# Transposing keys and values by 32x32 blocks on VectorE and DMA instead of by products with the identity on TensorE

## The chip, the cores and the metric

The kernel runs on one core of one Trainium2 chip, whose engines are called here PE (TensorE, products), PEld (its weight loads), DVE (VectorE), ACT (ScalarE), POOL (GpSimd) and SP (SyncE). Each runs its own list of instructions in order. SP computes nothing; it issues the transfers between DRAM and the on-chip memory SBUF, or inside SBUF, which 16 DMA engines carry out. PE writes to PSUM, eight banks that DVE and ACT can read. The metric is the time of one launch in device microseconds (us), the median over the runs; lower is better.

## The reference

One layer of a language model on a sequence of 4096 positions with width 1024, and a final normalisation. Two groups of heads share one input projection: 4 heads of gated linear attention (GLA, key width 64, value width 128) and 8 heads of RWKV-7 (width 64). The code below is cut to what the change touches, the names are the reference's.

```
h = rmsnorm(x, norm_w);  u = h @ w_in            # 4096 x 1024, 1024 x 3728
# GLA, in chunks:  scores and the state of each head
scores  = einsum('id,jd->ij', q * exp(b), k * exp(-b))     # causal
o       = scores @ v + (q * exp(b)) @ S
S       = exp(b_last) * S + (k * exp(b_last - b)).T @ v
# RWKV-7, per position t and head (S: value x key)
S = S * w_t + (S @ -kk_t) (kk_t * a_t)^T + v_t^T k_t
y = S @ r_t
y = groupnorm(y);  y = y + sum(r * k * r_k) * v
out = rmsnorm(x + concat(gla * silu(gate), y * silu(gate)) @ w_out)
```

A product on PE sums over the partition axis (the 128 rows of SBUF). Projections give q, k, v with channels as rows and positions as columns. For the states the sum runs over positions, so keys and values are needed the other way round, with positions as rows. These are the transposes that the change is about.

## The kernel before, in words

The sequence is cut into 8 blocks of 512 positions. In a block the 8 RWKV heads are 4 units of two heads (128 channels), the 4 GLA heads are 2 pairs of two heads; so there are 32 units and 16 pairs in all. Each unit has 8 chunks of 64 positions, each pair 4 chunks of 128.

The program is written as generators, called streams: x (loads and normalises a block of x), w (splits the weights at the start), a (the RWKV units up to their chains), i (the rest of a unit's triangular inverse), c (the chains over the chunks, which carry the state), p and g (GLA's projections and pairs), o (the output projection of a block). A recorder (class Engine, `call` at L626, `duo` at L685) writes down every instruction that a stream makes; in the profile almost all instructions therefore carry one of these two lines, and they are told apart by engine and tile names. A planner then gives each instruction a place on its engine: `first_guide` (L227) unpacks the table STARTS into one start time for each recorded step of each stream (COUNTS tells how many a stream has), `build` runs the streams in the order of these times, and `forward` and `backward` (L450, L518) lay the steps out with the durations of `cost` (L546), counting at most 8 transfers in flight. At the end the steps are emitted in the order of their starts, each engine's as one list. So the order of all engines hangs on that table, on the durations, and on what waits for what. All transfers named here are issued by SP from one list.

One unit (`rwkv_ab`, L1084) does this. It projects the key input (rk), makes the decays, the normalised key and kf (the key with its factor), and projects r. From these it builds bk: 128 channels x 8 chunks x 128 columns, which hold k and the removal key of a chunk side by side. The products of bk with de and do, masked, give DD and Nb, the small matrices of each chunk. Nb's diagonal 32x32 blocks go out to DRAM (nd) and back as F (f in the profile), POOL inverts them in 62 steps on Tc and tm, and they return over DRAM (td) into Nb. Stream i (`rwkv_i`, L1234) then finishes the inverse with Ta. Meanwhile the unit projects v and the gate rg. Then come the transposes:

- bk, L1201 to L1208: eight products with the identity into two PSUM banks, four each, and two ACT copies of 128x512 back over bk.
- v, L1209 to L1220: four products with the identity into one bank; there DVE takes the sum of each position and head (vm) and takes the mean off (with no mean over a head's values, y has none either, which the group norm asks for), and four ACT copies of 64x256 put the result into sv.

`rwkv_c` (L1256) is the chain over the 8 chunks: three small products of PE for a chunk, on ch, with ACT's copies us and uv between them, and at the end of each link DVE writes the state for the next chunk into sv (`sv<-ch`). It reads Nb, the transposed bk, and sv.

A GLA pair (`gla_pair`, L1399) makes the factors bc and ep (tiles gbc and gep), multiplies them into qi and ki, and transposes ki by four products with the identity and one ACT copy into kt, which is the buffer of bc (L1434 to L1439). It then multiplies kt with vt for the change of the state (pd), uses ep's buffer for the states (sm), and later reuses kt's and ki's buffers for the squares (rss).

The tiles ta, kf, E, v, rk and rn exist once each and pass from unit to unit; bk and sv exist twice, the projection weights wr and wg in a few buffers each, refilled from DRAM (wdr) all the time.

```
T.transpose(f4(pt[c // 4])[:, c % 4, :], bk[:, c, :], ident)                  # L1203, bk
T.transpose(pv[:, c].rearrange("p h t -> p (h t)"), v[:, P * c:P * c + P], ident)   # L1213, v
T.transpose(pt[:, c, :], ki[:, c, :], ident)                                  # L1437, GLA
```

## Time and profile before

| | |
|---|---|
| time, median of 3 runs | 2201.78 us (2199.61 to 2207.04) |
| span of the profiled execution | 2206.1 us |
| mean granted PE clock in it | 0.993 |
| busy, PE | 2119.0 us, 96% |
| busy, PEld | 1352.7 us, 61% |
| busy, DVE | 1711.7 us, 78% |
| busy, ACT | 1253.8 us, 57% |
| busy, POOL | 875.1 us, 40% |
| DMA queue q1, share of 16 engines | 50.8% |

The profiled execution's span, from its first to its last instruction, is 2206.1 us; its own launch time is not told apart from the three above, the nearest of which is 2207.04 us. A row of instruction groups reads: line, engine, operation, the tile written <- the tiles read, shapes, xcount | busy us in all, mean ns of one | idle us of the engine just before them, and what ended that idle time. A row of a stretch reads: start:end length, then for PE, PEld, DVE, ACT and POOL the busy us and the count of instructions, the granted clock, the DMA share and GB/s. A row of waits reads: engine and tile that wait <- what they wait for: us in all, count, the longest. A row of the timeline reads: start, duration, what ran. "SPq" is SP issuing a transfer, "DMA" its travel to the landing. The engines overlap, so the busy times of one say nothing yet about the time of the launch.

### The profile page before, as it was taken

Reading aid. Unit: us, or ns where it says so; the run is one execution under the profiler, and the core shown is the slowest. Engines: PE = TensorE matmul, PEld = TensorE weight load, DVE = VectorE, ACT = ScalarE, POOL = GpSimd, SP = SyncE. Lnnn points to the kernel's source line nnn. Section 1 sums busy time; section 2 is a strip of 40 time slices with the busy share of each in tenths; the row PEclk is TensorE's granted clock in tenths of the full one; section 3 lists DMA queues with packets and bytes.
Section 4 is the critical chain, followed back from the end, with each engine's and each line's share of the span. In section 5 each row is a group of like instructions: output and inputs, shape, how many; then the busy total and the mean of one; then the engine's idle time right before and its main releaser. Section 6 shows DMA issues by size and latency. Waiting matters only on the chain.

```text
span 2206.1 us, 75003 instructions
## 1 busy us (share of the span) xinstructions
PE 2119.0 (96%) x30680; PEld 1352.7 (61%) x30680; DVE 1711.7 (78%) x3802; ACT 1253.8 (57%) x3229; POOL 875.1 (40%) x2212
## 2 busy tenths in 40 slices
PE   7888999999999999999999999999999999999997
PEld 3555665566755657556575666656666566756664
DVE  7888969688784977867877886867878578785876
ACT  7766675564645546554654546545465465555452
POOL 3454233625244352335525354441543525254400
PEclk9999999999999999999999999999999999999999
DMA  6786556455344643456444654355544465345443
GB/s 201 230 249 205 182 160 178 141 177 167 91 123 142 184 141 98 115 145 188 138 114 116 183 154 129 101 131 165 164 117 124 127 190 160 90 117 140 130 123 97
DMA packets 275454, 326.90 MB, mean 148 GB/s; under 512 B 131572, under 2 KB 132772, under 8 KB 275108
## 3 DMA queue, kind: packets, MB, share of 16 engines
q1 hardware_dynamic: 275108, 322.10, 50.8%
q8 instruction: 240, 3.93, 0.8%
q14 instruction: 106, 0.87, 0.1%
HBM read 276.94 MB, written 45.05 MB: 146 GB/s over the span
## 4 chain that ended last, share of the span: by engine, by line
PE 66%; DVE 16%; DMA 9%; issue 2%; ACT 2%; SPq 2%; POOL 2%; DVEq 0%; POOLq 0%; ACTq 0%
PE bank L685 52%; PE bank L626 8%; PE ch L685 4%; DMA xr<-in_xT_dram 2%; SPq L626 2%; DVE DD L626 2%; DVE nta L626 1%; DVE bk L626 1%; PE y L626 1%; DMA rn<-bcda 1%; DMA x<-in_wt_dram 1%; PE y L685 1%; DVE mgg L626 1%; DVE x L626 1%; DVE Nb L626 1%
## 5 line engine op out<-in xcount | busy, mean ns | idle before, releaser
L685 PE MATMUL bank<-x,wr 128*64 128x512 f16 x6528 | 796.2, 380 | 7.2 <-ACT x L626 1.4
L626 POOL TENSOR_TENSOR tm<-Tc,f 128x60 f32<-128x60 f32 (+24 forms) x961 | 347.7, 362 | 589.0 <-DMA f<-nd 507.2
L685 PEld LDWEIGHTS <-wr 128*64 128x64 f16 x6528 | 356.1, 110 | 260.1 <-issue 22.1
L626 POOL TENSOR_TENSOR Tc<-Tc,tm 128x60 f32<-128x60 f32 (+24 forms) x961 | 358.2, 373 | 74.1
L685 PE MATMUL bank<-x,wg 128*64 128x512 f16 x3072 | 367.1, 381 | 3.0 <-DMA wg<-wdr 1.9
L685 PE MATMUL bank<-x,wo 128*64 128x512 f16 x2976 | 357.2, 380 | 0.0
L626 POOL TENSOR_TENSOR xacc<-xacc,xr 128x512 f32<-128x512 f32 x98 | 130.8, 1334 | 359.5 <-ACT xr L626 227.9
L685 PEld LDWEIGHTS <-wg 128*64 128x64 f16 x3072 | 169.4, 110 | 126.3 <-issue 5.0
L626 DVE SCALAR_TENSOR_TENSOR sv<-ch,PC,psd 64x64 f32<-64x64 f32 x434 | 122.5, 282 | 160.1 <-PE ch L685 140.6
L685 PEld LDWEIGHTS <-wo 128*64 128x64 f16 x2976 | 159.2, 110 | 112.4 <-issue 2.9
L685 PEld LDWEIGHTS <-x 128*64 128x64 f16 x6240 | 190.1, 111 | 20.8 <-issue 9.0
L685 PE MATMUL bank<-wg,x 128*64 128x128 f16 x6144 | 195.4, 220 | 4.6 <-DMA wg<-wdr 3.0
L626 ACT ACTIVATE psd<-sv,PC 128x128 f32<-128x128 f32 x248 | 98.9, 399 | 139.4 <-DVE sv L626 108.3
L626 ACT COPY uv<-ch 64x64 f32<-64x64 f32 x496 | 102.3, 206 | 76.5 <-PE ch L685 69.5
L626 ACT COPY us<-ch 64x64 f32<-64x64 f32 x496 | 102.2, 206 | 67.8 <-PE ch L685 57.7
L626 ACT ACTIVATE sa<-bank,mu_s 128x512 f32<-128x512 f32 x104 | 71.6, 689 | 73.5 <-PE bank L685 71.1
L626 DVE COPY_PREDICATED Nb<-mc,bank 64x512 f32<-64x512 uint8 x128 | 92.8, 728 | 13.1 <-PE bank L626 11.3
L626 POOL MEMSET Tc<- 32x8 f32 (+1 forms) x160 | 24.2, 151 | 186.1 <-DMA td<-Tc 180.7
L626 DVE COPY_PREDICATED DD<-mc,bank 64x512 f32<-64x512 uint8 x128 | 93.3, 731 | 2.3
L685 PEld LDWEIGHTS ch<-uv,bk 128*64 128x64 f32 x992 | 66.1, 137 | 44.1 <-ACT uv L626 10.9
L685 PEld LDWEIGHTS ch<-us,Nb 128*64 128x64 f32 x992 | 65.4, 137 | 43.0 <-ACT us L626 11.0
L685 PEld LDWEIGHTS ch<-sv,DD 128*64 128x64 f32 x992 | 65.0, 136 | 40.0 <-DVE sv L626 7.3
(348 smaller groups left out, 3611.8 us busy)
## 6 DMA issues: line engine op xcount, KB each, us to landing
wr<-wdr SPq DMA_DIRECT2D x256, 256.0 KB
wg<-wdr SPq DMA_DIRECT2D x184, 256.0 KB
xr<-in_xT_dram SPq DMA_DIRECT2D x176, 256.0 KB
wo<-wdr SPq DMA_DIRECT2D x128, 256.0 KB
f<-nd SPq DMA_DIRECT2D x128, 128.0 KB
x<-in_wt_dram SPq DMA_DIRECT2D x29, 512.0 KB
wdr<-wo SPq DMA_DIRECT2D x25, 512.0 KB
out_dram<-mgg SPq DMA_DIRECT2D x33, 256.0 KB
```

The source lines that it names most:

```text
L626: put(t0, self.name, d, lag, cols, tiles, tab, outs, ins, lambda: f(*a, **kw))
L685: nc.tensor.matmul(x, lhsT=l, rhs=y, start=start, stop=stop)
```

## The change

Keys and values are transposed without PE. DVE's block transpose turns every 32x32 block of a tile and leaves the block where it stands; transfers then carry the blocks to where they belong.

- bk: right after the masked products of the unit, one block transpose of the whole bk (128x1024) into sv's buffer, four transfers of 128 KB from there to DRAM (kd, in pieces of 32 numbers), and one of 512 KB from DRAM over bk.
- v: one block transpose (128x512) into kf's buffer, and eight transfers of 32 KB inside SBUF into ta's buffer. The sum and the removal of the mean now work there instead of in PSUM, and two ACT copies of 64x512 put the result into sv.
- ki of GLA: one block transpose into ep's buffer, four transfers of 64 KB to DRAM (gd) and one of 256 KB over bc's buffer.
- `cost` gets a duration for the larger block transposes, and the tables COUNTS and STARTS are replaced.

```diff
--- before.py
+++ after.py
@@ -53,143 +53,140 @@
 PASSES = 5
 PUT_OFF = 1.0
 ROUNDS = (LOOKS,) * 1
-COUNTS = ((('d', 0), 19), (('d', 1), 19), (('d', 10), 19), (('d', 11), 19), (('d', 12), 19),
+COUNTS = (('a', 9713), ('c', 3379), ('e', 109), ('g', 1736), ('i', 1184), ('init', 38), ('o', 2464),
 STARTS = (
...
 )
 GUP = 2.0 ** 19
 DECAY = math.exp(-0.5)
@@ -560,6 +557,8 @@
                     runs = 0.126
                 elif n == 256 and half:
                     runs = 0.122 if op == "transpose" else 0.09
+                elif op == "transpose":
+                    runs = n * 0.00037
                 elif n == 512 and half:
                     runs = 0.115
                 elif op == "tensor_scalar" and few > 1:
@@ -1157,6 +1156,14 @@
             rel("r")
             hot.pop()
 
+            sv = sb(un, [P, NC, 2, 64], F32, "sv", 2)
+            sw = sv.rearrange("p c e t -> p (c e t)")
+            V.transpose(sw, bk.rearrange("p c t -> p (c t)"))
+            kd = sb(dr, [4, 32, NC, 4, 32], F32, "kd", 2)
+            for a in range(4):
+                D.dma_start(kd[:, :, :, a].rearrange("b i c t -> i c b t"), sw[32 * a:32 * a + 32].rearrange("p (c b t) -> p c b t", b=4, t=32))
+            D.dma_start(bk.rearrange("p c t -> p (c t)"), kd.rearrange("b i c a t -> (b i) (c a t)"))
+
             F = sb(rt, [P, 1024], F32, "f4", 1).rearrange("p (k t) -> p k t", k=32)
             nd = sb(dr, [4, NC, 32, 32], F32, "nd", 2)
             for q in range(4):
@@ -1198,26 +1205,20 @@
                 stat_mm(pst, bones, r)
                 add_bonus(pst[:, 0:P], *bonus.pop())
                 rel("r")
-            pt = yield from need("r", 2)
-            for c in range(NC):
-                T.transpose(f4(pt[c // 4])[:, c % 4, :], bk[:, c, :], ident)
-                if c == 3:
-                    yield now[0]
-            for i in range(2):
-                S.copy(bk[:, 4 * i:4 * i + 4, :], f4(pt[i]))
-            rel("r")
             yield after(v)
-            sv = sb(un, [P, NC, 2, 64], F32, "sv", 2)
-            pv = (yield from need("r")).rearrange("p (c h t) -> p c h t", c=4, h=2)
-            for c in range(4):
-                T.transpose(pv[:, c].rearrange("p h t -> p (h t)"), v[:, P * c:P * c + P], ident)
+            x, vt = tA("kf"), tA("ta")
+            V.transpose(x, v)
+            vt = f3(vt)
+            for a in range(4):
+                for s in range(2):
+                    o = 64 * (a < 2) + 32 * s
+                    D.dma_start(vt[o:o + 32, :, 32 * (a % 2):32 * (a % 2) + 32],
+                                x[32 * a:32 * a + 32].rearrange("p (c s t) -> p c s t", s=2, t=32)[:, :, s])
             vm = sb(rt, [P, 8, 1], F32, "vm", 1)
-            pu = pv.rearrange("p c h t -> p (c h) t")
-            V.tensor_reduce(vm, pu, op=ALU.add, axis=AX.X)
-            V.scalar_tensor_tensor(pu, vm.broadcast_to((P, 8, 64)), -1.0 / 64, pu, ALU.mult, ALU.add)
-            for k, q in enumerate((lo, hi)):
-                for e, o in enumerate((hi, lo)):
-                    S.copy(sv[o, k::2, e, :], pv[q, :, e, :])
+            V.tensor_reduce(vm, vt, op=ALU.add, axis=AX.X)
+            V.scalar_tensor_tensor(vt, vm.broadcast_to((P, 8, 64)), -1.0 / 64, vt, ALU.mult, ALU.add)
+            for e, o in enumerate((hi, lo)):
+                S.copy(sv[o, :, e, :], vt[o])
             units[u] = (DD[u % NBUF], nb, sv, bk, PC, bv, tg)
             done["A"] += 1
 
@@ -1430,14 +1431,15 @@
             done["GE"] += 1
             yield lambda: done["GV"] > n
             ki, qi, vt = g["ki"], g["qi"], g["vt"]
-            kt, sm = bc, ep
+            sm = ep
             yield after(ki)
-            pt = f4((yield from need("G")))
-            for c in range(4):
-                T.transpose(pt[:, c, :], ki[:, c, :], ident)
-            S.copy(kt, pt)
-            rel("G")
-            yield after(kt, vt)
+            xt, kt = ep.rearrange("p c t -> p (c t)"), bc
+            V.transpose(xt, ki.rearrange("p c t -> p (c t)"))
+            gd = sb(dr, [4, 32, 4, 4, 32], F32, "gd", 2)
+            for a in range(4):
+                D.dma_start(gd[:, :, :, a].rearrange("b i c t -> i c b t"), xt[32 * a:32 * a + 32].rearrange("p (c b t) -> p c b t", b=4, t=32))
+            D.dma_start(kt.rearrange("p c t -> p (c t)"), gd.rearrange("b i c a t -> (b i) (c a t)"))
+            yield after(bc, vt)
             pd = f4((yield from need("G")))
             for c in range(4):
                 duo(pd[:, c, :], [pd[h, c, :] for h in (lo, hi)], [kt[:, c, h] for h in (lo, hi)], [vt[:, c, P * e:P * e + P] for e in range(2)], True, True)
@@ -1469,7 +1471,7 @@
             for c in range(4):
                 for e, q_ in two:
                     T.matmul(po[e][:, c, :], lhsT=sm[q_, c, :], rhs=qi[q_, c, :], start=False, stop=c == 3)
-            os_, rss = [tG("go", 2) for _ in range(2)], [t.rearrange("p c t -> p (c t)") for t in (kt, ki)]
+            os_, rss = [tG("go", 2) for _ in range(2)], [t.rearrange("p c t -> p (c t)") for t in (bc, ki)]
             for e in range(2):
                 S.copy(os_[e], po[e].rearrange("p c t -> p (c t)"))
                 S.activation(rss[e], os_[e], AF.Square)
```

In the orders below a row is the line, the operation, the tile written <- the tiles read, the shape, and xN where N alike stand in a row. The numbers behind a tile's name are those of the buffers; bank_0_... are PSUM banks.

PE at a change of block, before: between the products of an output tile or projection (bank<-x) stand the four for the pair's ki, then small products of the same pair (gtwo) and the unit (bones), then the four for v, and the inverse's (Nb, Ta).

```order
L685 MATMUL bank_0_187<-x_0_1_0_84,wr_212 64x512
L626 MATMUL bank_0_188<-gbc_231,gtwo_101 32x128 x4
L626 MATMUL bank_0_188<-ki_249,gtwo_101 32x128 x4
L626 MATMUL bank_0_186<-r_200,bones_105 32x128 x4
L626 MATMUL bank_0_190<-ident_76,v_201 128x128 x4
L626 MATMUL bank_0_189<-Nb_0_137,Ta_266 32x32 x16
```

PE of the change, around the same sums over gbc and ki:

```order
L684 LDWEIGHTS wr_212
L684 MATMUL bank_0_186<-x_0_2_0_85,wr_212 64x512
L625 MATMUL bank_0_189<-gbc_231,gtwo_101 32x128 x4
L625 MATMUL bank_0_189<-ki_253,gtwo_101 32x128 x4
L684 LDWEIGHTS wr_212
L684 MATMUL bank_0_186<-x_0_2_0_85,wr_212 64x512
```

The products with ident are gone, here and everywhere; in the program's whole list these are the only products of PE that differ in number, 448 of them. Behind the sums over ki the projection goes on at once.

SP of the change, at a change of block. `ta<-kf` are v's eight pieces, `kd<-sv` are bk's four, nd belongs to the inverse, wr and wg are weights, xr is x:

```order
L625 DMA ta_198<-kf_199 32x8x32 x2
L625 DMA wr_214<-wdr_0_155 128x1024
L625 DMA xr_221<-in_xT_dram 128x512
L625 DMA wr_212<-wdr_0_147 128x1024
L625 DMA wr_215<-wdr_0_155 128x1024
L625 DMA kd_245<-sv_243 256x4x32
L625 DMA ta_198<-kf_199 32x8x32 x2
L625 DMA wg_241<-wdr_0_166 128x1024
L625 DMA wr_213<-wdr_0_147 128x1024
L625 DMA xr_222<-in_xT_dram 128x512
L625 DMA nd_247<-Nb_0_137 32x8x32 x2
L625 DMA kd_245<-sv_243 256x4x32
```

The pieces of one v are spread over the list, with weights, x, bk's pieces and the inverse's between them. SP issues 2317 transfers in all where it issued 1821.

DVE of the change, the end of the same v. nva, nya and nta are a chain of small steps (an inverse square root), vm and the row behind it are the sum and the removal of the mean of v, sv<-ch is a link of another unit's state chain, and mgg belongs to the output:

```order
L625 TENSOR_SCALAR nva_207<-bank_0_185 128x128
L625 TENSOR_SCALAR nya_235<-nva_207 128x128
L625 TENSOR_TENSOR nta_209<-nya_235 128x128
L625 SCALAR_TENSOR_TENSOR nta_209<-nta_209,nva_207 128x128
L625 SCALAR_TENSOR_TENSOR nya_235<-nta_209,nya_235 128x128
L625 TENSOR_TENSOR nta_209<-nya_235 128x128
L625 SCALAR_TENSOR_TENSOR nta_209<-nta_209,nva_207 128x128
L625 SCALAR_TENSOR_TENSOR nya_235<-nta_209,nya_235 128x128
L625 TENSOR_REDUCE vm_258<-ta_198 128x8
L625 SCALAR_TENSOR_TENSOR ta_198<-vm_258,ta_198 128x512
L625 SCALAR_TENSOR_TENSOR sv_243<-ch_271,PC_229,psd_273 64x64 x2
L625 SCALAR_TENSOR_TENSOR mgg_0_92<-bank_0_188,iv_287,xr_222 128x512
```

The sum of v stands on DVE's list behind all eight transfers of the pieces above (it reads ta, which they fill); before, it read the bank that PE's four products had filled. The block transposes of this v and of a bk (not shown) stand 21 and 20 rows ahead of it.

269 lines of the change are left out of this document (133 added, 136 removed).

## The prediction

> **What bounds the kernel now.** I read the page first, then the busy time by stretch, then the waits. The page's head, its table of engines, the transfers and the chain of waits:
>
> ```profile
> span 2206.1 us, 75003 instructions
> PE 2119.0 (96%) x30680; PEld 1352.7 (61%) x30680; DVE 1711.7 (78%) x3802; ACT 1253.8 (57%) x3229; POOL 875.1 (40%) x2212
> q1 hardware_dynamic: 275108, 322.10, 50.8%
> PE 66%; DVE 16%; DMA 9%; issue 2%; ACT 2%; SPq 2%; POOL 2%; DVEq 0%; POOLq 0%; ACTq 0%
> ```
>
> PE is busy for 96% of the span and carries 66% of the chain; the transfers fill half of the 16 DMA engines' time. An average hides stages, so next the busy time in three stretches (length, then PE, PEld, DVE, ACT, POOL with their instructions, the granted clock, the DMA share and GB/s):
>
> ```profile
> 0.00:207.00 207.00, 169.58 (x2158) 100.91 (x2160) 179.96 (x500) 144.66 (x281) 85.77 (x178) 0.96 0.73 221
> 207.00:2139.00 1932.00, 1898.46 (x27850) 1221.03 (x27846) 1490.34 (x3205) 1087.52 (x2885) 789.36 (x2034) 1.00 0.50 142
> 2139.00:2206.00 67.00, 50.99 (x683) 30.80 (x678) 41.45 (x99) 21.64 (x65) 0.00 (x0) 0.94 0.34 106
> ```
>
> In the long middle PE rests only 1932 - 1898.5 = 33.5 us: there PE's work sets the time, at a granted clock of 1.00. In the first 207 us PE rests 37 us, and DVE (87% busy) and transfers (73%) are the fuller resources. The last 67 us are the latency of the end.
>
> **What leaves PE.** The transposes against the identity, by group, then the same products alone by stretch:
>
> ```profile
> L626 PE MATMUL bank<-ident,bk 128*128 128x128 f32 x256 | 37.4, 282 | 1.6 <-DVE DD L626 1.6
> L626 PE MATMUL bank<-ident,v 128*128 128x128 f32 x128 | 20.3, 281 | 1.5 <-DVE om L626 1.1 <-DVE DD L626 0.3
> L626 PE MATMUL bank<-ident,ki 128*128 128x128 f32 x64 | 10.5, 286 | 0.0
> ...
> 207.00:2139.00 1932.00, 61.86 (x420) 44.58 (x420) 0.00 (x0) 0.00 (x0) 1.00 0.50 142
> sum 2206.00, PE 66.23 PEld 47.53 DVE 0.57 POOL 0.50; mean PE 13.25 PEld 9.51 DVE 0.11 POOL 0.10
> ```
>
> All 448 go: 8 for bk and 4 for v in each of 32 units, 4 for ki in each of 16 pairs. They cover 66.2 us of PE, 61.9 of them (420 pieces: 30 units, 15 pairs) in the middle, 4.4 before it, none after. Matmuls overlap their neighbours, so busy time overstates what a removal frees. The timeline shows the true step, from the start of a group to the start of the next:
>
> ```profile
> 1013.46 1.09 PE L626 MATMUL bank<-ident,bk 128*128 128x128 f32 x8
> 1014.48 0.34 PE L685 MATMUL ch<-sv,DD 128*64 128x64 f32 x4
> ...
> 1029.85 0.66 PE L626 MATMUL bank<-ident,v 128*128 128x128 f32 x4
> 1030.44 0.42 PE L626 MATMUL bank<-rn,bones 128*32 128x128 f32 x8
> ...
> 1036.99 0.66 PE L626 MATMUL bank<-ident,ki 128*128 128x128 f32 x4
> 1037.58 1.16 PE L626 MATMUL bank<-qi,ki 64*128 64x128 f32 x16
> ```
>
> Eight cost 1.02 us, four cost 0.59. A unit gives back 1.61 us and a pair 0.59; in the middle 30 x 1.61 + 15 x 0.59 = **57.2 us**, between that and the 61.9 of busy time. I take 57.2. The order shows no other change of PE's work: all other products are there in the same numbers.
>
> **What DVE and ACT get.** The nearest rows:
>
> ```profile
> L626 DVE STREAM_TRANSPOSE Ta<-Nb 32x256 f32<-32x256 f32 x64 | 27.6, 431 | 12.6 <-DMA Nb<-td 11.5
> L626 DVE COPY Ta<-bank 128x256 f32<-128x256 f32 x32 | 13.5, 421 | 5.9 <-PE bank L626 5.5
> L626 DVE TENSOR_REDUCE vm<-bank 128x8 f32<-128x512 f32 x32 | 22.0, 687 | 11.7 <-PE bank L626 11.4
> L626 DVE SCALAR_TENSOR_TENSOR bank<-vm,bank 128x512 f32<-128x512 f32 x32 | 22.1, 691 | 0.6
> L626 ACT COPY bk<-bank 128x512 f32<-128x512 f32 x64 | 35.6, 585 | 5.0 <-PE bank L626 4.6
> L626 ACT COPY sv<-bank 64x256 f32<-64x256 f32 x128 | 46.9, 366 | 20.8 <-DVE bank L626 13.4 <-DVE iv L626 3.3 <-DVE invs L626 2.4
> L626 ACT COPY uv<-sv 64x512 f32<-64x512 f32 x62 | 38.1, 614 | 9.8 <-PE ch L685 9.3
> ```
>
> A block transpose of 256 columns takes 431 ns. From 256 to 512 columns a plain step grows by (691 - 421) = 270 ns; with that slope 512 columns take 0.70 us and 1024 take 1.24 (431 + 3 x 270); in plain proportion to 431 they take 0.86 and 1.72. Per unit (1024 for bk, 512 for v) 1.94 to 2.58 us, per pair 0.70 to 0.86: in all 32 x 1.94 + 16 x 0.70 = 73 to 96 us. I take 85, the middle, since neither row is nearer. The mean and its removal stay two steps of about 0.69 us each on v, from SBUF now. DVE goes to 1711.7 + 85 = 1797 us, still under PE's 2119 - 66 = 2053. ACT loses 35.6 for bk, 46.9 for sv and 16 copies of ki (like bk's, 9.4), and gains 64 copies of 64x512 like uv's (39.3): 53 us less, of no worth, since ACT stands idle anyway. On the path these steps count nothing while PE has other work queued; without that cover they cost up to the 96.
>
> **What the transfers get.** 13 transfers a unit (4 + 1 for bk, 8 for v) and 5 a pair: 496 more. They move 50 MB in 229,376 pieces of 128 bytes plus 21 MB of long rows. Two stretches of 1 and 20 us, the first nearly all short pieces, the second a change of block; then one round trip through DRAM, the transfers that DVE waits for now, and the products of the V projections:
>
> ```profile
> DMA packets 653, 0.11 MB, mean 111 GB/s; under 512 B 636, under 2 KB 636, under 8 KB 653
> q1 hardware_dynamic: 653, 0.11, 74.4%
> ...
> DMA packets 3248, 5.22 MB, mean 261 GB/s; under 512 B 889, under 2 KB 889, under 8 KB 3243
> q1 hardware_dynamic: 3243, 5.15, 88.8%
> ...
> 1037.74 2.93 DMA bcda<-nya
> 1041.25 3.29 DMA rn<-bcda
> ...
> DVE crs L626 <- DMA crs<-bcdc: 8.0, 6, 3.1
> DVE rn L626 <- DMA rn<-bcda: 7.2, 9, 1.8
> DVE bv L626 <- DMA bv<-bcdb: 4.8, 5, 2.8
> ...
> L685 PE MATMUL bank<-wg,x 128*64 128x128 f16 x6144 | 195.4, 220 | 4.6 <-DMA wg<-wdr 3.0 <-issue 1.5
> ```
>
> 0.744 x 16 us over 653 packets is 18 ns for a short piece, long ones counted in. 229,376 x 18 ns / 16 = 258 us of each engine; 21 MB at 5.15 MB in 17.8 busy us adds 73. The share rises from 51% to about 66% (331 of 2206 more): not full on average, fuller at a change of block, where it is 89% already. The transposed bk is read first by the unit's state chain, behind the triangular inverse that fills most of POOL's 875 us, 27 a unit; the transposed ki is read by PE behind both V projections of its pair, 195.4 / 16 = 12 us. Both have cover; the direct price is nothing, and without it one landing of about 3 us each, 48 times.
>
> v has less cover. The piece of SP's order shown with the change lies at a change of block. From the first to the eighth piece SP issues 24 transfers there (12 of its rows are shown), weights among them. SP's pace before, in two stretches (start, time, transfers), first and last row of each; and what PE now waits for that link of the state chain which DVE writes:
>
> ```profile
> 1055.27 0.33 SPq L626 DMA_DIRECT2D wr<-wdr  x1
> ...
> 1064.06 0.92 SPq L626 DMA_DIRECT2D Nb<-td  x2
> ...
> 999.65 0.40 SPq L626 DMA_DIRECT2D wr<-wdr  x1
> ...
> 1018.70 0.35 SPq L626 DMA_DIRECT2D xr<-in_xT_dram  x1
> ...
> PE ch L685 <- DVE sv L626: 1.7, 2, 1.4
> ```
>
> 18 transfers in 9.7 us is 0.54 each; 21 in 19.4 us is 0.92. So 24 take 13 to 22 us, plus 2.9 to land: 16 to 25. DVE's order at the same place, also shown there, has the reduction that waits for all eight pieces, and directly behind it the second step on v and a link of another unit's state chain (sv<-ch), for which PE waits. Between v's block transpose and the reduction DVE has 20 rows; at its pace in the middle (1932 us over 3205) that is 12 us of cover. The pieces come 4 to 13 us late. In the other units of the middle DVE has 16 to 39 rows in between and SP 13 to 24, off the change of block at the quicker pace. So I count 4 us at each of 7 changes of block, 28 us of DVE, and of that about a third for PE, **10 us**: PE has products queued between two links, and though DVE waits 20 us for crs, rn and bv today, PE waits only 1.7 us for sv. Bounds: nothing, and 7 x 13 = 91.
>
> **The sum.** Start: PE sheds 4.4 us but DVE, the fuller engine, gains two units and a pair, 4.6 to 6.0 us; I take 0, from -4 to +6. Middle: -57 + 10. End: no transpose stands there, but the last unit's v now makes a round of transfers; 0, up to +7. 2206.1 - 57.2 + 10 = 2159 on the profiled execution's span. The page does not say which run it profiled; the nearest is 2207.04, 0.9 us above the span. The median of the three runs is 2201.78, 4.3 us under the span, so **2155 us**.
>
> One page speaks against the change: the Trainium skill, DMA: Bandwidth & Descriptors, section Rules for kernel authors, tells authors to transpose in flight with the hardware transpose and not by a plain transfer with a rearranged access pattern, with a 19x difference. Here DVE turns the blocks, and the transfers move whole 128-byte rows; the row of 18 ns a packet does not bear the rule out. By this figure of the Trainium skill, an estimate, the 512 KB of one bk at 290 GB/s would take 34 us instead of 1.8, and 32 of them over 1000 us of transfers.
>
> **The rivals.**
> 1. The whole saving: no new stall, busy time in full, 2206.1 - 66.2 - 4.3 = 2136. For it: DVE's present waits for transfers hardly reach PE. Against: neighbours overlap, and the start is not PE's. Chance 0.15.
> 2. Slower: the reduction of v holds DVE's queue, and the state chain behind it holds PE. At 13 us for each of 7 changes, 91 us: 2206.1 - 57.2 + 91 - 4.3 = 2236. It decides once PE loses more than 8 us a change (57.2 / 7). For it: 24 transfers on one queue in order, at the slow pace. Against: that pace holds only while weights and x come in together. Chance 0.12.
> 3. No change: DVE becomes the limit wherever it is fullest. If its added 85 us cost PE time in proportion to DVE's 77% share of the middle (1490 of 1932), 65 us come back: 2206.1 - 57.2 + 65 - 4.3 = 2210, or near 2202 if a little less does. Against: DVE's idle 442 us in the middle. Chance 0.08.
> 4. The transfers become the bound: each short piece costs what a mixed packet costs at the change of block, 0.888 x 320 us over 3243 = 88 ns. 229,376 x 88 / 16 = 1262 us on top of 1121 (50.8%) and 73: 2456 us. Against: the 18 ns of the row above. The Trainium skill's rule cited above, on DMA: Bandwidth & Descriptors, points to this rival. Chance 0.03.
>
> **How the numbers follow.** My forecast has 0.62. About 0.3% is what a measurement of this kernel can tell from no change, 6.6 us. Faster: 0.62 + 0.15 = 0.77. Same: 0.08, the third. Slower: 0.12 + 0.03 = 0.15. The likeliest case alone spans 2138 to 2190. The range goes from 2134, just under the full saving, to 2200, with rivals 2 to 4 and a little below left out.
>
> **What would show it.** Right: PE's busy time falls by about 66 us, PE's rest in the middle stays under 50 us, a block transpose of 1024 columns takes 1.2 to 1.7 us, the queue's share stands near 66%, and DVE's waits for ta are under 40 us in all. Wrong: a wait of DVE for ta, or of PE for sv or DVE's chain, of more than 60 us (rival 2); DVE above 90% in the middle with PE's rest over 90 us (rival 3); a share above 85% with weights late (rival 4). A fall of PE's busy time much under 61 us would mean that the products were cheaper than the timeline says.

## The result, and the profile after

The change made the kernel slower: 2251.95 us as median of 4 runs (2247.67 to 2266.42) against 2200.7 us before (4 runs, 2197.53 to 2207.04). The ratio is 1.0241, with a 95% interval of 1.0202 to 1.0279. The forecast was 2155 us. So 51 us were lost where 46 were expected to be won, and the question is where some 97 us went. One of the four runs, that of 2266.42 us, had a mean granted clock of 0.933 where the others had 0.977 to 0.980; without it the ratio would be 1.022.

The page of the profiled execution (2247.67 us by its own time) has these lines; below them stand the three stretches, the first two cut at the same times as before, and then the mean granted clock of this execution and of the one before:

```profile
span 2245.7 us, 74902 instructions
PE 2089.1 (93%) x30232; PEld 1323.0 (59%) x30232; DVE 1773.4 (79%) x3882; ACT 1210.4 (54%) x3085; POOL 904.3 (40%) x2212
q1 hardware_dynamic: 518564, 372.46, 59.8%
PE 56%; DVE 17%; DMA 14%; SPq 6%; issue 3%; ACT 3%; POOL 1%; DVEq 0%; ACTq 0%; POOLq 0%
```

```profile
0.00:207.00 207.00, 160.04 (x2071) 94.75 (x2073) 171.55 (x475) 139.57 (x263) 77.04 (x178) 0.94 0.78 234
207.00:2139.00 1932.00, 1838.44 (x26825) 1169.64 (x26819) 1522.61 (x3196) 1025.18 (x2690) 827.25 (x2034) 0.99 0.60 163
2139.00:2245.00 106.00, 90.59 (x1354) 58.59 (x1350) 79.24 (x213) 45.62 (x132) 0.00 (x0) 0.95 0.45 129
```

```profile
core 0: 2245.7 us, clock 0.980
```

```profile
core 0: 2206.1 us, clock 0.993
```

Three things are to be seen. First, PE's rest in the middle went from 33.5 us to 1932 - 1838.4 = 93.6 us; over the whole span it went from 2206.1 - 2119.0 = 87.1 to 2245.7 - 2089.1 = 156.6 us, which is 69.5 us more. In the chain of waits PE fell from 66% to 56%, and DMA and SP's issuing together rose from 11% to 20%.

Second, PE's busy time fell by 29.9 us only, though 66.2 us of products had gone: the products that stayed took 36.3 us longer. The clock tells much of it: the share of the span that was not granted went from (1 - 0.993) x 2206.1 = 15 us to (1 - 0.980) x 2245.7 = 45 us, 30 us more. That is the most that it can explain, since some of it fell on PE's rests. So the sum is -66.2 + 36.3 + 69.5 = 39.6 us, the difference of the two spans.

Third, DVE and the queue did what was forecast, or less. The block transposes by group:

```profile
L625 DVE STREAM_TRANSPOSE sv<-bk 128x1024 f32<-128x1024 f32 x32 | 39.4, 1232 | 0.2
L625 DVE STREAM_TRANSPOSE kf<-v 128x512 f32<-128x512 f32 x32 | 22.7, 708 | 0.6
L625 DVE STREAM_TRANSPOSE gep<-ki 128x512 f32<-128x512 f32 x16 | 11.3, 708 | 0.4
L625 DVE TENSOR_REDUCE vm<-ta 128x8 f32<-128x512 f32 x32 | 21.8, 682 | 33.6 <-DMA ta<-kf 24.2 <-DMA wr<-wdr 6.4 <-issue 1.5
```

They take 73.4 us in all, and the last row shows that the sum of v waits 24 us in all for the moved blocks. Who waits longer than before is told by the waits, PE's and then DVE's, after the change:

```profile
PE bank L684 <- DMA wg<-wdr: 26.7, 18, 4.2
PE ch L684 <- DVE sv L625: 17.1, 20, 2.8
PE ch L684 <- ACT uv L625: 9.5, 9, 2.9
PE ch L684 <- ACT us L625: 9.3, 10, 2.8
```

```profile
DVE vm L625 <- DMA ta<-kf: 24.2, 10, 3.5
DVE Ta L625 <- DMA Nb<-td: 20.5, 13, 5.4
DVE crs L625 <- DMA crs<-bcdc: 18.2, 9, 3.8
DVE go L625 <- DMA gbc<-bcdh: 13.6, 6, 5.1
DVE rn L625 <- DMA rn<-bcda: 13.3, 10, 3.9
```

and of PE before, the rows that the prediction did not show:

```profile
PE bank L685 <- DMA wg<-wdr: 4.9, 5, 1.9
...
PE ch L685 <- ACT uv L626: 4.5, 6, 1.3
PE ch L685 <- ACT us L626: 4.3, 7, 1.8
```

The waits that grew are not mainly those for the moved blocks. They are for transfers that were there before: weights (wg, from 4.9 to 26.7 us), the broadcasts crs and rn (from 8.0 and 7.2), the returning inverse (Nb, from 11.5). Summed over all rows of the view, DVE's waits for transfers went from 40 to 125 us, of which ta is 24. No single one is large.

No row of PE, DVE or ACT waits for bk<-kd or gbc<-gd, the landings of the transposed bk and ki. But their first legs are waited for: ACT may not write into sv and gep while the transfers to kd and gd still read them, and SP issues bk<-kd only when kd has landed, and holds all that stands behind it in its list:

```profile
ACT sv L625 <- DMA kd<-sv: 11.4, 4, 4.2
ACT gep L625 <- DMA gd<-gep: 10.5, 3, 4.6
SPq L625 <- DMA kd<-sv: 18.8, 15, 3.8
```

The chain of waits shows how one such stall is made. A piece of it at a change of block (start, duration, what):

```profile
1049.86 0.60 SPq L625
1050.50 0.62 SPq L625
1051.21 0.55 SPq L625
1051.80 0.58 SPq L625
1052.48 1.50 SPq L625
1054.03 2.28 DMA f<-nd
...
1064.13 2.44 DMA bcdx<-nyg
1066.59 0.33 SPq L625
1067.01 5.44 DMA wg<-wdr
1072.49 2.90 PE bank L684 x15
```

SP issues one transfer right behind the other: by its timeline 31 in the 21.5 us up to this weight block, 8 of them added ones (ta, kd, bk, gd) of 0.43 to 0.63 us each. Shortly before the end it stands 0.75 us for the landing of bcdx, a transfer that was there before, and the weight behind it in the list stands too. The weight then takes 5.4 us to land, and PE waits for it. What PE's rest then does to its clock stands in four stretches of about 3.4 us around that place, and in PE's products with wg in the last two of them:

```profile
1066.40:1069.90 3.50, 3.50 (x44) 2.38 (x40) 2.08 (x3) 1.53 (x4) 2.88 (x8) 1.00 0.90 204
1069.90:1073.30 3.40, 1.19 (x16) 0.68 (x13) 1.46 (x3) 0.72 (x2) 2.92 (x7) 1.00 0.99 330
1073.30:1076.70 3.40, 3.40 (x20) 1.47 (x16) 3.39 (x5) 1.52 (x4) 3.01 (x6) 0.50 0.41 104
1076.70:1080.10 3.40, 3.40 (x34) 1.77 (x32) 3.32 (x6) 0.62 (x1) 3.01 (x6) 1.00 0.63 186
```

```profile
L684 PE MATMUL bank<-x,wg 128*64 128x512 f16 x20 | 4.0, 583 | 0.0
```

```profile
L684 PE MATMUL bank<-x,wg 128*64 128x512 f16 x34 | 3.9, 386 | 0.0
```

In the second stretch PE was busy for 1.19 of 3.40 us, while the queue was at 0.99. In the third the granted clock was 0.50, and the same product took 583 ns instead of 386: PE did 20 products where it does 34 in the next stretch. So a rest of 2.2 us cost a further 14/34 x 3.4 = 1.4 us. In the whole trace the clock was at 0.50 in 19 spells of 3.4 to 10.2 us, in that of before in 5. In the 3.4 us ahead of each of the 19 PE was busy for 1.75 us or less; eight other stretches with as little were not followed by a spell. PE was busy for 68.4 us inside the spells, before for 19.4; if 14/34 of the 49 us more were lost, as in the stretch shown, that is 20 us. The Trainium skill, TensorE: Matmul & The Clock Gate, section HAM oscillation, tells of this with waits for transfers as the cause, and prices the spells at half speed at half their length. By that rule, an estimate, the 49 us lost 25. So 20 to 25 of the 36.3 us by which the products grew are the clock's, and the rest is not assigned.

### The profile page after: what moved, and what is told of

Read it like the earlier page. It is cut to its first block, busy times and chain, and to the rows that moved or that the text cites. A ratio compares the mean times of both kernels' runs of the same rounds, so it can differ in the third digit from the quotient of the medians.

```text
span 2245.7 us, 74902 instructions
## 1 busy us (share of the span) xinstructions
PE 2089.1 (93%) x30232; PEld 1323.0 (59%) x30232; DVE 1773.4 (79%) x3882; ACT 1210.4 (54%) x3085; POOL 904.3 (40%) x2212
## 3 DMA queue, kind: packets, MB, share of 16 engines
q1 hardware_dynamic: 518564, 372.46, 59.8%
## 4 chain that ended last, share of the span: by engine, by line
PE 56%; DVE 17%; DMA 14%; SPq 6%; issue 3%; ACT 3%; POOL 1%; DVEq 0%; ACTq 0%; POOLq 0%
PE bank L684 44%; PE bank L625 6%; SPq L625 6%; PE ch L684 3%; DMA xr<-in_xT_dram 2%; DMA wg<-wdr 2%; DVE DD L625 2%; DVE x L625 1%; DMA ta<-kf 1%; PE y L625 1%; DVE Nb L625 1%; PE y L684 1%; DVE sv L625 1%; DVE bk L625 1%; DVE mgg L625 1%
## 5 line engine op out<-in xcount | busy, mean ns | idle before, releaser
L684 PE MATMUL bank<-x,wr 128*64 128x512 f16 x6528 | 810.1, 384 | 18.0 <-DMA wr<-wdr 6.2
L625 POOL TENSOR_TENSOR tm<-Tc,f 128x60 f32<-128x60 f32 (+24 forms) x961 | 367.2, 382 | 591.8 <-DMA f<-nd 469.5
L625 POOL TENSOR_TENSOR Tc<-Tc,tm 128x60 f32<-128x60 f32 (+24 forms) x961 | 368.9, 384 | 74.1
L684 PE MATMUL bank<-x,wg 128*64 128x512 f16 x3072 | 373.3, 381 | 9.9 <-DMA wg<-wdr 6.8
L684 PEld LDWEIGHTS <-wo 128*64 128x64 f16 x2976 | 163.7, 111 | 121.8 <-issue 6.6
L684 PE MATMUL bank<-wg,x 128*64 128x128 f16 x6144 | 210.7, 223 | 22.5 <-DMA wg<-wdr 20.0
L684 PEld LDWEIGHTS <-x 128*64 128x64 f16 x6240 | 200.6, 113 | 42.8 <-issue 28.9
```

Of the source, the lines that this page charges most:

```text
L625: put(t0, self.name, d, lag, cols, tiles, tab, outs, ins, lambda: f(*a, **kw))
L684: nc.tensor.matmul(x, lhsT=l, rhs=y, start=start, stop=stop)
```

## The experiments

Ratios are to the kernel before, with 95% intervals, each against runs of that kernel on the same chip; a difference of ratios is turned into us with 2201 us, and by the intervals a difference of two rows is good to about 10 us. Kernels of the first part are the change itself with something left out when the instructions are emitted: the plan and the order of all else are the change's, so nothing is planned anew.

| kernel | ratio | against the change |
|---|---|---|
| the change | 1.0241 [1.0202, 1.0279] | |
| without all added transfers | 0.9806 [0.9777, 0.9835] | -96 us |
| all transfers small | 0.9898 [0.9867, 0.9930] | -75 us |
| without v's | 0.9980 [0.9965, 0.9995] | -57 us |
| without bk's | 0.9930 [0.9912, 0.9949] | -68 us |
| without ki's | 1.0120 [1.0092, 1.0148] | -27 us |
| long pieces | 1.0091 [1.0068, 1.0113] | -33 us |
| nobody reads what arrives | 1.0136 [1.0100, 1.0171] | -23 us |
| issued by ACT | 1.0231 [1.0192, 1.0270] | -2 us |
| without bk's and v's, first two units of a block | 1.0079 [1.0062, 1.0095] | -36 us |
| the same, last two units | 0.9977 [0.9958, 0.9996] | -58 us |

**Is it the transfers?** The theory was that the 496 added transfers make the loss; the rival was the new order, or a fuller DVE. In the loop that emits the steps, the transfers are passed over:

```diff
         for s in sorted(steps, key=lambda s: (start[s.n], s.n)):
+            if s.eng == "D" and s.io in (("ta", "kf"), ("kd", "sv"), ("bk", "kd"), ("gd", "gep"), ("gbc", "gd")):
+                continue
             s.f()
```

> The change's program and order with its 496 added transfers left out (so the transposed bk, v and ki never arrive; the state's decay PC is scaled by 1e-6 so that the numbers stay finite, the work is otherwise the same). DVE's block transposes and the order of everything else stay. Theory A (the added transfers on SP's list make the loss): the 97 us between the 2252 measured and the 2155 forecast come back, 2135 to 2165. Rival B (the new order, or DVE's block transposes with DVE fuller, make it): the time stays above 2210.

It took 2161.77 us, 0.9806 of before: 96 us come back, of the 97 that were missing. DVE's block transposes and the new order stay in this kernel, so they are not the bulk of the loss; the page has DVE fuller than in the change, and PE at rest for 2163.5 - 2062.2 = 101 us:

```profile
span 2163.5 us, 74090 instructions
PE 2062.2 (95%) x30232; PEld 1315.2 (61%) x30232; DVE 1783.7 (82%) x3882; ACT 1206.8 (56%) x3085; POOL 918.0 (42%) x2212
```

PE's busy time is 56.8 us under that of before, and its rest 14 us over it. Summed over the rows of the views, PE waits 45 us for DVE where it waited 33 before, and DVE 62 us for transfers where it waited 40. So the new order with the fuller DVE has a price of its own, some 14 us that the transfers do not make.

**Issuing, or the load?** The same transfers were issued at the same places, each with 128 bytes.

```diff
+            if s.eng == "D" and s.io in MOVED:
+                o, i = s.aps
+                few = (slice(0, 1),) * (len(o.shape) - 1) + (slice(0, 32),)
+                nc.sync.dma_start(o[few], i[few])
```

> All 496 transfers are issued at their places and with their waits, but each moves 128 bytes at most (what they leave out is not transposed; PC scaled as in the run without them). Theory A1 (SP's time to issue and the waits in its list): stays near the change, 2225 to 2255. Rival A2 (the load on the DMA engines, 230,000 short pieces): falls to the time of the run without transfers, 2135 to 2175.

2180.86 us, between the two forecasts and nearer to the rival's: 0.9898 - 0.9806, 20 us of the 96, stay when the transfers are issued and move next to nothing. The waits for landings have not gone (DVE still waits 10.4 us for ta), and it is not quite the same issuing. All of SP's issues take 1075 us here, 1213 in the change and 827 before, and the tile view shows that a transfer of kd took 286 ns of SP (median) with 128 bytes, 428 ns with 32 rows and 589 ns with 1024 pieces (least, median, longest in ns; first the change, then small, then long pieces):

```profile
L625 SPq DMA_DIRECT2D kd<-sv x128: 575/589/1798, 59.3 to 2144.9; - x128
```

```profile
L1771 SPq DMA_DIRECT2D kd<-sv x128: 220/286/443, 59.4 to 2068.8; - x128
```

```profile
L1773 SPq DMA_DIRECT2D kd<-sv x128: 313/428/1728, 60.0 to 2113.7; - x128
```

**Which part?** v's, bk's and ki's transfers were left out singly, with the condition of the first kernel cut to (ta, kf), to (kd, sv) and (bk, kd), and to (gd, gep) and (gbc, gd).

> Only v's 256 transfers are left out (the values are then wrong, the rest stays). A1: they are 52% of the added issues and 177 us of 351 us of added issue time on SP, and the reduction of v no longer waits: half to two thirds of the 97 us come back, 2187 to 2205. If the price is the data (A2): v moves 8 MB of the 71, and 65,536 of the 229,376 short pieces, so under a third comes back, 2222 to 2245.

> Only bk's 160 transfers are left out (bk stays untransposed, PC scaled by 1e-6). A1: a third of the issues, 97 us of 351 of the issue time: 25 to 40 us come back, 2212 to 2227. A2: bk has 131,072 of the short pieces and most of the long rows, so well over half comes back, 2170 to 2195.

> Only ki's 80 transfers are left out (ki's transposed copy is then wrong). Leaving out v's took 51 us off the change and bk's 63, all together 90: so the parts overlap. In proportion to short pieces (32,768 of 229,376) 13 us come back, in proportion to issues (80 of 496) 15: both say 2235 to 2245. If GLA's pair has cover, as the prediction had it, nothing: 2248 to 2256.

v gave back 57 us (2200.58), bk 68 (2188.65), ki 27 (2232.85), 152 in all where leaving out all three gives 96. So the parts are not added up: in this order each one's transfers cost more while the others' are there. bk's came out as the load would have it and v's as the issuing would, so both count; ki is not free, though no row waits for the landing of its transposed copy. (The transfers move 50 MB in all, as the page of the kernel with ACT below shows; the 71 of the first expectation count the long rows twice, and of the prediction's "50 MB in 229,376 pieces" the pieces are 29.) Each part costs more here than the products that it removes (33, 19 and 9 us by the timeline).

**Short pieces, or bytes?** The transfers of kd, ta and gd move whole rows.

```diff
-                D.dma_start(kd[:, :, :, a].rearrange("b i c t -> i c b t"), sw[32 * a:32 * a + 32].rearrange("p (c b t) -> p c b t", b=4, t=32))
+                nc.sync.dma_start(kd.rearrange("b i c a t -> (b i) (c a t)")[32 * a:32 * a + 32], sw[32 * a:32 * a + 32])
```

> The same 496 transfers at the same places with the same bytes, but those of kd, ta and gd move whole rows (32 rows of 4, 1 and 2 KB) instead of pieces of 128 bytes, so what they leave out is the right place of each block (bk, v and ki are wrong; PC scaled by 1e-6). 229,376 short pieces become 22,528 rows. Theory B1 (the short pieces are the price, on the DMA engines or in SP's issuing): close to the run with small transfers, 2170 to 2195. Rival B2 (the bytes): most of the loss stays, 2220 to 2255.

2225.26 us: 33 us go with the short pieces, on the DMA engines or in SP's issuing (1139 us in all here), and 1.0091 - 0.9898, 42 us, remain for the bytes and for those who wait for them. Both theories were half right. The queue's share was 57.3% here and 59.8% in the change.

**SP's list?** All 496 were issued by ACT.

```diff
-                s.f()
+                nc.scalar.dma_start(*s.aps)
```

> All 496 transfers whole, with the right result, but issued by ACT at the places that the planner gave them on SP; SP's list is then as long as before (1821). ACT was busy 54%. Theory C1 (SP's list is what is late: 386 us of added issuing, and one waiting transfer holds all behind it): 2165 to 2200, less what ACT loses. Rival C2 (the DMA engines' load): stays at 2235 to 2265. Rival C3 (ACT's own copies on the chain of the state, held by the waits of the transfers): slower than the change, above 2265.

2254.09 us, no better. The page of its slowest run (2269.55 us) and PE's waits:

```profile
q1 hardware_dynamic: 275108, 322.10, 48.7%
q10 hardware_dynamic: 243456, 50.36, 11.3%
```

```profile
PE bank L687 <- DMA wg<-wdr: 20.0, 12, 3.9
PE ch L687 <- ACT us L628: 17.8, 22, 2.1
...
PE ch L687 <- ACT uv L628: 13.8, 16, 3.3
```

The second queue shows the load by itself: 11.3% of 16 engines' span, 256 us of each. With SP's list as short as before, weights are still late (20.0 us), as the load would have it; but ACT's copies us and uv are later too (17.8 and 13.8 us, against 9.3 and 9.5), so SP's relief may have been paid back there, and this run alone does not clear SP. The Trainium skill, DMA: Bandwidth & Descriptors, section Issuing engines are not separate DMA queues, says that transfers of all issuers run on the same 16 engines and that another issuer saves only the time to issue. The run agrees in that the two queues together filled 60.0% of the engines, as the one did in the change (59.8%).

**The load, or those who read?** What brings the blocks home was sent to a scratch instead.

```diff
-                    D.dma_start(vt[o:o + 32, :, 32 * (a % 2):32 * (a % 2) + 32],
+                    nc.sync.dma_start(junv[o:o + 32, :, 32 * (a % 2):32 * (a % 2) + 32],
...
-            D.dma_start(bk.rearrange("p c t -> p (c t)"), kd.rearrange("b i c a t -> (b i) (c a t)"))
+            nc.sync.dma_start(junk, kd.rearrange("b i c a t -> (b i) (c a t)"))
```

> The change's program, order and all 496 transfers with their sources, waits for the sources, bytes and 128-byte pieces, but what brings the blocks home (ta<-kf, bk<-kd, gbc<-gd) goes to a scratch in DRAM that nobody reads; so no engine waits for a landing of the change (bk, v, ki are wrong; PC scaled by 1e-6). Theory D1 (issue and load make other transfers late, weights, broadcasts and the inverse's): 2225 to 2260, like the change. Rival D2 (the engines that wait for the moved blocks, v's sum at the head of DVE's list above all): near the run with small transfers, 2175 to 2200.

2237.07 us: 23 us belong to bringing the blocks home. In the waits of the change that is v's sum. The transfers home must also wait until the tile that they fill is free, which the scratch spares them, and v's pieces go to DRAM here instead of staying in SBUF; that is in the same difference. 1.0136 - 0.9898, 52 us, lie between this kernel and the one with small transfers. Weights and broadcasts are as late as in the change, though nothing waits for a block to come home:

```profile
PE bank L688 <- DMA wg<-wdr: 29.3, 16, 4.3
```

```profile
DVE rn L629 <- DMA rn<-bcda: 18.8, 11, 4.7
```

So the 96 us are about 20 for small transfers issued and awaited, 52 for their full shape and bytes (the short pieces have a large part of it), and 23 for bringing the blocks home; the three add up by construction, since each difference starts where the last one ends. The 52 are not the lateness of other transfers alone. Between the two kernels PE's waits for transfers grow from 14 to 37 us, but its waits for ACT grow from 33 to 58, where ACT itself is held 23 us by kd and gd instead of 7, and SP's issues take 1222 us instead of 1075.

**The other side.** The kernel before was given 496 transfers of 128 bytes, spread evenly over SP's list.

```diff
             s.f()
+            if s.eng == "D":
+                n += 1
+                if n * 496 // 1821 > (n - 1) * 496 // 1821:
+                    k = n * 496 // 1821
+                    nc.sync.dma_start(extra[k:k + 1], ident[0:1, 0:32])
```

> The kernel before with 496 transfers of 128 bytes added to SP's list, spread evenly and waiting for nothing (from the identity to a scratch in DRAM that nobody reads). If issuing alone costs what the run with small transfers showed (2181 - 2162 = 19 us in the change's order), 10 to 25 us slower than before. If only the places in bursts at a change of block cost, within 6 us of before.

2226.48 us, ratio 1.0091 [1.0074, 1.0108]: 20 us, as in the change's order. Nothing in the kernel before was changed or planned anew, so a transfer more on SP's list costs 0.04 us here even where it stands apart, waits for nothing and moves 128 bytes. SP's issues took 957 us instead of 827.

**One part alone.** In the kernel before, with its own order table, one part was moved, and the planner placed the new steps (the change's lines take the place of the old ones, and the count of steps is carried on: `nth[cur[0]] += 10` for bk).

> The kernel before, in its own order table, with bk alone moved to DVE and transfers (the 256 products and 64 copies gone, 32 block transposes and 160 transfers added; their places come from the planner). Saving by the timeline 32 x 1.02 = 33 us. Cost: 63 us if bk's price is what leaving it out gave back, 40 if the three parts' 141 us are scaled to the 90 of all together: 2213 to 2236. Rival (the price comes only when all three fill the queue): 2180 to 2198.

> The kernel before, in its own order table, with v alone moved (128 products gone, 256 transfers added). Saving 32 x 0.59 = 19 us. Cost 33 to 51 us, as for bk: 2220 to 2238. Rival (only all together fill the queue): 2187 to 2203.

> The kernel before, in its own order table, with ki alone moved (64 products gone, 80 transfers added). Saving 16 x 0.59 = 9 us. Cost 13 to 19 us (19 = what leaving ki's transfers out gave back): 2209 to 2217. Rival (only all together fill the queue): 2196 to 2204.

bk alone took 2204.23 us, 0.9998 [0.9982, 1.0015] of before: the 33 us of products and the price cancel; it lay between the two forecasts. v alone took 2226.41 (1.0096 [1.0064, 1.0128]), with 256 transfers for 19 us of products, ki alone 2217.57 (1.0054 [1.0037, 1.0071]). None of the three parts is a gain by itself, and none came as low as the rival had it (only all together fill the queue). With the saved products the prices are 33, 40 and 21 us, 94 together, about as much as all three cost in the change; so here, other than in the change's order, the parts do add up, as far as plans can be compared (see the control below).

**Where in a block?** bk was moved in 14 units where the queue is quieter (first two units of a block), or fuller (last two), and bk and v in the quieter ones.

```diff
+            moved = b >= 1 and p < 2          # the other kernel: b <= NB - 2 and p >= 2
+            if moved:
+                ... the block transpose and the five transfers of bk
```

> The kernel before, in its own order table, with bk moved to DVE and transfers only in the 14 units that come where the queue is quiet (the first two units of blocks 2 to 8; in the trace of before the queue's share in the 20 us behind such a unit's masked products is 0.33 to 0.71, mostly under 0.5). Saving 14 x 1.02 = 14 us. Theory E1 (the price is paid where the queue is near full already): 2190 to 2198, faster than before. Rival E2 (the price goes with the number of transfers wherever they stand: bk alone cost as much as it saved): within 5 us of before, 2201 to 2211.

> The same for 14 units that come where the queue is fuller (the last two units of blocks 1 to 7; share 0.54 to 0.82). Saving 14 us. E1: the saving is used up and more, 2208 to 2225. E2: within 5 us of before, 2201 to 2211.

> bk and v moved in the 14 quiet units only, all else as before. Saving 14 x 1.61 = 23 us. E1: 2184 to 2196. E2, with the prices of bk alone (33 us for 32 units) and v alone (40 us for 32): 14/32 of 73 = 32 us, 2210 to 2220.

> A control: the kernel before, its order table unchanged, with nothing moved; the planner alone is told that a block transpose of 256 columns takes 0.13 us longer, which shifts some 2800 rows of PE's list (bk alone shifted 5135, ki alone 2986). It tells how much of the differences of the kernels with one part alone is the new plan. If plans of this kind are worth nothing: 2201 to 2211. If they are worth as much as ki alone lost: above 2215.

In the quieter units it took 2206.07 us (0.9999 [0.9985, 1.0013]), in the fuller ones 2221.34 (1.0065 [1.0048, 1.0081]). With 14 us of products gone in both, the price was 14 us at the quieter places and 28 at the fuller ones. bk and v in the quieter units gave 2206.54 (0.9999 [0.9989, 1.0010]), a price of 23 us for 23 us of products. The control without any move gave 2200.94 (0.9971 [0.9958, 0.9985]): a new plan alone is worth 6 us, so differences of that size between planned kernels prove nothing; the 15 us between the two places are more than that, though one control does not bound what a new plan can do. In the profiled run of the quieter units the saving is gone on PE itself:

```profile
PE 2118.6 (96%) x30568; PEld 1350.5 (61%) x30568; DVE 1728.0 (78%) x3816; ACT 1237.5 (56%) x3201; POOL 877.8 (40%) x2212
```

```profile
core 0: 2209.4 us, clock 0.986
```

112 products fewer, and PE is as busy as before (2119.0): the clock was at 0.986 instead of 0.993, (0.014 x 2209.4) - (0.007 x 2206.1) = 15 us, the most that the clock can have cost. The other runs of this kernel had 0.985 to 0.989, those of before beside them 0.989 to 0.993.

So that no plan is mixed in, the same question was put to the change's own order, with bk's and v's transfers left out by the place of the unit (`if u % 4 < 2: continue`, and `u % 4 >= 2`):

> The change's program and order, without a new plan; bk's and v's 208 transfers are left out for the first two units of every block (16 of 32; ki's stay; PC scaled by 1e-6). Leaving out all transfers gave back about 96 us (0.9806 against 1.0241), ki's alone 27; if half of the transfers is worth half, 35 to 45 come back: ratio 1.004 to 1.009. If the price is paid at the fuller places, in the ratio 1 to 2 that the kernels with 14 units moved showed (14 and 28 us): 20 to 30 come back, 1.010 to 1.015.

> The same for the last two units of every block, which stand at the change to the next block. Half for half: 35 to 45 us back, ratio 1.004 to 1.009. Fuller places: 45 to 60 back, 0.997 to 1.004.

First units 36 us back (2224.87), last units 58 (2203.46): the last units carry 62% of it, and the first are not free. With ki's 27 the three make 121 us, more than the 96 of all. So the place counts. That it is the fuller queue alone is not shown: in the change's trace the share in the 20 us behind the block transpose of bk is 0.67 on average for the first units and 0.73 for the last, which also lie at the change of block.

## Why the prediction was wrong, point by point

- **The removal from PE: right in kind, some 14 us too large.** Where the transfers were left out, the time fell by 43 us (0.9806); the term was 57.2. PE's busy time fell by 56.8 us, which is near the term by luck: the forecast for busy time was 66, and of the 9 us between a part is the clock of that run, 0.989 instead of 0.993. PE's rest grew by 14 us, from 87 to 101, which the term had not. In the change itself busy time fell by 29.9 us only; that was my sign for cheaper products, but the products that stayed grew, in good part by the clock.
- **Block transposes, DVE: right.** 1.23 us and 0.71 us, at the lower ends of 1.24 to 1.72 and 0.70 to 0.86; 73 us in all where I took 85. With the transfers left out DVE at 82% left PE waiting 13 us more for it; that is far from the 65 of rival 3.
- **The transfers' load: the size was over-estimated, the price missed.** The step that failed stands in "What the transfers get": a share of 66%, "not full on average", "Both have cover; the direct price is nothing". The sum had 10 us for all 496 transfers, and they cost 96; with the 43 that the removal gave, that is the loss of 53 us in the ratio 1.0241. The cover was there, since nothing waited for the landings of bk and ki; what failed is the step from cover to a price of nothing. The share came out at 59.8%, so the queue had less to do than forecast. A short piece took less than the 18 ns: a stretch of the change that has almost nothing else gives 0.811 x 16 x 1.4 us / 1316 = 14 ns:

```profile
DMA packets 1316, 0.17 MB, mean 124 GB/s; under 512 B 1311, under 2 KB 1311, under 8 KB 1316
q1 hardware_dynamic: 1316, 0.17, 81.1%
```

  But I asked only whether the moved blocks have cover, and not what 496 transfers do to the others on the same queue. PE waited 8 us for these others (weights, broadcasts, the inverse's trips) before, summed over its rows, 11 in the change's order without the added transfers, and 34 with them. I also left out who must wait before a source is written again: ACT, held 22 us by kd and gd, while PE's waits for ACT went from 32 us without the transfers to 53 with them. Load, longer issuing and ACT's waits together are the 52 us; the runs do not tell them apart.
- **SP's issuing: not priced.** I worked out SP's pace to say when v's last piece lands, and gave the 496 issues no price of their own. Small ones cost 20 us, in the change's order and in that of before; the change's take longer to issue, and how much that adds is not told apart from the load.
- **v's sum at the head of DVE's list: the mechanism is there, its size in the range.** DVE waited 24 us for ta, under the 28 forecast, and bringing the blocks home is worth 23 us where I took 10. Rival 2 (2236 us) came nearest in time, but by its own sign, more than 60 us of waits for ta or of PE for sv, it did not happen: PE's for sv grew from 1.7 to 17.1.
- **The clock: not seen at all.** The row of the middle stretch had shown 1.00, and I took PE's rest as the only price of a stall. 20 to 25 of the 36 us by which the remaining products grew are spells at half speed behind rests. The stall of 2.2 us shown above cost 3.6.
- **Rival 4 had the right place and a wrong price**: weights late at a change of block, where the queue was indeed full for a few us (0.90 and 0.99 in the stretches above), but at 60% over the span and at 14 ns a piece, not 88. The Trainium skill's rule that I cited there (DMA: Bandwidth & Descriptors, Rules for kernel authors) does not hold here in its factor: by the 34 us that it gave for one bk there would be over 1000 us of transfers, and the added load was 256 us of each engine. Its advice, the transpose in flight, no run tried.
- **The chances.** No rival's sign was met in full (of rival 3's, PE's rest in the middle was over 90 us, 93.6, but DVE was at 79% there; rival 4's share above 85% held for moments only), and the kernel was still 97 us from the forecast: the loss came in many pieces of 1 to 4 us at many waits. A list of rivals, each with one large wait, does not hold that case; the chance of slower, 0.15, was too low for a change that adds 27% to the issues of a list on which a kernel with 96% of PE busy depends. One of the signs of being right did fail plainly: PE's rest in the middle was to stay under 50 us.

What stays open: how the 52 us divide between short pieces that hold the engines, SP's longer issue of them (kd 589 instead of 428 ns) and ACT's waits for kd and gd; the kernel with long pieces changes all three. And the kernel with ACT as issuer does not tell what SP's list alone is worth, since ACT was held in turn.

## What to carry to other kernels

In a kernel whose plan is tight, price an added transfer by what it does to the transfers already there, not by whether its own result is needed soon: in this kernel 0.04 us for each small issue and 0.15 us more for shape, load and landing (96 us for 496), and 1.6 to 2 times as much in the last units of a block as in the first. Ask also who must wait until the transfer has read its source. Count a stall on PE half as much again and more if it leaves PE idle for most of a 3.4 us stretch, because the clock was then mostly halved for the next one. And test such a trade by leaving out one side of it at the emission, with the order kept, before the whole is tuned: the transfers' share of the result was plain from one run.

## What the runs showed of the hardware that was not expected

- 128 bytes in a transfer or 128 KB in 1024 pieces: SP's issue took 286 ns or 589 ns (kd, median). So the shape of a transfer is paid on the issuing list as well as on the DMA engines.
- PE at 1.19 of 3.40 us busy was enough for the next 3.4 us to run at a clock of 0.50; a full 3.4 us of rest was not needed. Each of the 19 spells of this trace followed 3.4 us in which PE was busy for 1.75 us or less, and eight stretches with as little were followed by none.
- 496 transfers that move 128 bytes each, depend on nothing and are read by nobody cost 20 us of 2201 (1.0091 [1.0074, 1.0108]) in a kernel whose queue was at 51%.
- A block transpose of 128x1024 in f32 took 1232 ns and one of 128x512 708 ns, that is about 1.0 ns a column and 0.18 us for the instruction.
